# A hybrid decoder step on one core: first gMLP pair by plain products, output gates that leave PSUM without the heads, and work moved at two seams of the program

## The chip, the core and the metric

The kernel runs on one core of a Trainium2 chip. Times are device microseconds of one execution. The profile's names of the engines are used: PE (TensorE, matmuls and transposes), DVE (VectorE), ACT (ScalarE), POOL (GpSimd) and SP (SyncE, which here only issues DMAs). Each engine executes its instructions in the order of the program. "The clock" is the TensorE clock that was granted, which has two levels, 1.2 and 2.4 GHz, shown as 0.5 and 1.0.

## What is computed

One layer of a decoder trunk for 1024 prompt tokens and 64 sample tokens (8 sequences of 8), all in float32, D = 1024. The tokens are normalised and shifted by adaLN; one input projection feeds three branches; their gated outputs are projected, merged by sigmoid gates and projected once more. The reference, cut down:

```python
h = rmsnorm(x) * (1 + scale) + shift
z = h @ w_in + b_in                      # split into the columns named below
y_A = chunk_gmlp(u, v)                   # u * (causal mixing of rmsnorm(v)), 4 groups of 128 channels
y_B = sink_attention(q, k, v)            # window 128, 8 heads, 2 kv heads, sinks
y_C = sigmoid(o) * groupnorm(mlstm(conv(q, k), v, i, f))   # 4 heads of 128
y   = [y_b * silu(gate_b) for b in (A, B, C)]
m   = sum(sigmoid(merge_b) * (y_b @ w_b) for b in (A, B, C))
out = x + adaLN_gate * (m @ w_out)
```

It also returns the new keys and values of the window, the convolution's tail, the mLSTM states (C, n, m) and the normalised v of the samples.

## The kernel before, in words

**Products.** The 1088 tokens lie along the free dimension, the channels on the partitions, in 8 tiles of 128. A float32 product is made of three matmuls per tile of 128 rows, since each operand is split in a high and a low part (hh and hlo are h's; `w_split` and L124/L125 split weights: ACT casts the high part, DVE subtracts for the low one). A product over the whole of K = 1024 takes 24 matmuls for a piece of columns. PSUM results stand in three pools: pg (3 banks), pk (3) and pu (2). `gt` hands out temporary tiles of 128 x 384 from five buffers.

**Stage one, up to 349 us.** adaLN, h, then the mLSTM. While the four heads (`head`) run, PE fills its gaps with the products of the output gates: per head h, three chunks (384, 384 and 320 tokens) for o and three for g. `ev_o` (L785 to L787) takes Tanh of PSUM by ACT and multiplies it into `hn[h]`, the head's normalised output, by DVE. `ev_g` (L791 to L796) takes a second Tanh by ACT, then DVE multiplies the PSUM chunk itself into hn and the Tanh behind it. So an o chunk's bank is free once ACT has read it, and a g chunk's bank only when hn is there. At the end of a head DVE makes r out of dd (L736 to L740, with `rsqrt` L160 to L163 on POOL) and scales `num` by it (L741); PE transposes num, and ACT makes hn from that (L750). The states C_p and C_s go out by DMAs on POOL's queue (L694, L722), ahead of the rsqrt.

**Stage two, 359 to 600 us.** Nine `kv_tile`s, each a product of 24 matmuls of 256 columns into a pg bank, evicted by DVE into kn and vB (L921, L922). Then the attention: 20 steps (16 for prompts, 4 for samples), whose phases are interleaved on PE by hand (PLAN). Between them `filler` issues the products of the queries, of gMLP's v, and of `bg_chunk` (the silu gate of branch B, 12 chunks). A dict `tail` hangs more work on the steps: `t_first` (steps 0 to 3), `t_second` (11 to 18), `t_third` (22 to 25), `a_scale` (18: 36 ACT instructions that scale vn for the mixing), `mix(0)` to `mix(3)` (21, 22, 25, 25: causal mixing matrices times vn on PE, evicted by DVE, L1265).

**Stage three, 600 to 1079 us.** The gMLP pairs, their gates, the projections and merge gates. A pair is two column blocks of 128 of w_in times h. `seven` makes the 2 x 2 blocks (two halves of K, two halves of the tokens) of such a pair's four outputs by 7 products instead of 8, a Strassen scheme: products run over sums of halves of h (T tiles: `t_first` makes T5, `t_second` T6, `t_third` T4, and `t_in_place`, L1508 to L1514, T7 in the place of a half of h) and over sums of weight blocks (`comb`, L1366, by DVE). A product is 12 matmuls of 288 and 12 of 256 columns, two pieces of half the tokens. `items` is the list that runs here; `prepare` loads and splits the weights of an item five items ahead (LEAD). The first pair is item 0 to 7, behind `t_in_place`.

**Stage four, 1079 us to the end.** The output projection and the residual. It is not touched.

Of the kernel before, what the change touches and what calls it, by code (L numbers as in the profile page):

```python
# [38 lines left out]
def trunk_kernel(ctx: ExitStack, tc: tile.TileContext, I, O):  # L39
# [411 lines left out]
    with tc.tile_pool(name="cph", bufs=1, side="right", reuse_waits="tile") as c1:  # L451
# [166 lines left out]
        def head(h):  # L618
# [75 lines left out]
            nc.gpsimd.dma_start(O["C_p"][0, 0, h], Cp[:, 0:128])  # L694
# [14 lines left out]
            for b2 in range(2):  # L709
# [12 lines left out]
                nc.gpsimd.dma_start(O["C_s"][0, bs_, h].rearrange("b d e -> d b e"), Cs[b2][:, :, 0:128])  # L722
# [16 lines left out]
            rsqrt(r3, r2, 128)  # L739
# [76 lines left out]

    keep = ExitStack()
    k1 = keep.enter_context(tc.tile_pool(name="keep", bufs=1, side="right", reuse_waits="tile"))
    pe = ctx.enter_context(ExitStack())
    with tc.tile_pool(name="bph", bufs=1, side="right", reuse_waits="tile") as b1:  # L820
# [43 lines left out]
        ps = pk()  # L864
        tr(ps[:, 0:128], mT.rearrange("p a t -> p (a t)"))
        tr(ps[:, 128:160], mN.rearrange("p a h t -> p (a h t)"))
        mm(ps[:, 160:162], sel4.rearrange("p a h t -> p (a h t)"), snk4, True, True)
        V.tensor_copy(smask[:, 0:128], ps[:, 0:128])
        V.tensor_copy(smask[:, 160:192], ps[:, 128:160])
        scol = bt([128, 2], "scol")  # L870
        V.tensor_copy(scol, ps[:, 160:162])
        nscol = bt([128, 2], "nscol")
        V.tensor_scalar(nscol, scol, -1.0, None, ALU.mult)
# [32 lines left out]
        vB = slot("y7", [128, 9, 2, 64], name="vB")  # L906
# [103 lines left out]

        class Prompt:
# [12 lines left out]
            def s(self):  # L1024
# [60 lines left out]
        class Sample:  # L1085
# [19 lines left out]
            def s(self):  # L1105
# [108 lines left out]
        def t_next(x, q, k, kk, b, prev, to, c):  # L1214
            def v(t):
                return t[:, c].bitcast(F32)

            V.tensor_tensor(x, v(half(hh, kk, b)), v(TT[prev, k][0]), ALU.subtract)
            V.tensor_tensor(x, x, v(TT[prev, k][1]), ALU.subtract)
            V.tensor_tensor(x, x, v(half(hlo, kk, b)), ALU.add)  # L1220
# [560 lines left out]
```

## Time and profile before

| | |
|---|---|
| three runs | 1212.57, 1214.16, 1215.2 us, median 1214.16 |
| the profiled execution | 1213.49 us, its span 1211.8, so 1.7 us lie around the span |
| mean granted clock | 0.981 |
| busy: PE, DVE, ACT, POOL | 1162.9 us (96%), 790.1 (65%), 484.9 (40%), 77.5 (6%) |
| PE instructions | 8900 |

PE is busy nearly throughout, so a change counts by what it does to PE: fewer or more matmuls, less or more waiting, and the clock at which they run. What another engine does counts where PE waits for it. The rows behind the change show the waits.

### The profile page before, as it was taken

The numbers are of one execution on the slowest core, as the hardware profiler recorded it, in microseconds if no ns is written. First come the engines' busy times: TensorE is split into PE (matmuls) and PEld (weight loads), VectorE is DVE, ScalarE is ACT, GpSimd is POOL, SyncE is SP. The second block draws the span as 40 slices with busy tenths as digits, with TensorE's granted clock in tenths as the row PEclk, the third lists the DMA queues.
The fourth block names the chain that finished last, engine by engine and source line by source line (L and its number), as shares of the span: only waits on it lengthen the run. The fifth ranks groups of instructions, "written<-read, shape, count | busy, mean of one in ns | idle before, by whom it ended". The sixth has DMA issues, their size and how long they took to land.

```text
span 1211.8 us, 23137 instructions
## 1 busy us (share of the span) xinstructions
PE 1162.9 (96%) x8900; PEld 1113.5 (92%) x8900; DVE 790.1 (65%) x1887; ACT 484.9 (40%) x1215; POOL 77.5 (6%) x111
## 2 busy tenths in 40 slices
PE   5899999999979999999979999999999999999998
PEld 2699999999969998888878999999999999999998
DVE  3577877755465677776698784655766676668333
ACT  4443454433332377896243432333333343236000
POOL 2100001011022110010100000000000000000000
PEclk8999999999989999999988999999999999999999
DMA  9731222233222210213233246423544354466322
GB/s 306 230 88 36 73 67 79 58 106 102 80 66 68 69 40 23 71 41 99 61 87 106 81 129 203 149 82 96 169 111 112 110 167 127 127 205 195 99 90 74
DMA packets 150774, 129.74 MB, mean 107 GB/s; under 512 B 13614, under 2 KB 140214, under 8 KB 150649
## 3 DMA queue, kind: packets, MB, share of 16 engines
q1 hardware_dynamic: 142984, 118.96, 33.5%
q0 software_dynamic: 2240, 7.08, 1.7%
q10 hardware_dynamic: 5440, 2.23, 0.7%
q8 instruction: 70, 1.15, 0.4%
q14 instruction: 40, 0.32, 0.1%
HBM read 99.39 MB, written 29.82 MB: 107 GB/s over the span
## 4 chain that ended last, share of the span: by engine, by line
PE 50%; DVE 5%; ACT 3%; issue 1%; DMA 1%; SPq 0%; ACTq 0%; DVEq 0%
PE pg L85 21%; PE pk L85 17%; PE pu L85 12%; ACT vn L1255 1%; DVE prod L1372 1%; DMA raw<-in_w_out_dram 0%; ACT Sm L1044 0%; PE pu L89 0%; DMA mgr<-dmg 0%; DVE comb L1366 0%; DVE ml L1580 0%; DVE wo L1372 0%; DVE tx L1512 0%; ACT Sm L1052 0%; DVE sA L1265 0%
## 5 line engine op out<-in xcount | busy, mean ns | idle before, releaser
L85 PE MATMUL pg<-hl,hl 128*128 128x256 f32 (+3 forms) x904 | 278.1, 308 | 0.9 <-DVE hl L389 0.7
L85 PE MATMUL pg<-hh,hl 128*128 128x384 f32 (+1 forms) x912 | 238.9, 336 | 2.5 <-DVE hh L388 1.5
L85 PE MATMUL pg<-hl,hh 128*128 128x256 f32 (+1 forms) x1008 | 179.6, 285 | 0.1
L85 PEld LDWEIGHTS pg<-hl,hl 128*128 128x128 f32 x904 | 171.5, 190 | 4.0 <-DVE hl L389 2.7
L85 PEld LDWEIGHTS pg<-hh,hl 128*128 128x128 f32 x912 | 162.1, 190 | 6.8 <-DVE hh L388 2.9
L85 PEld LDWEIGHTS pg<-hl,hh 128*128 128x128 f32 x1008 | 151.9, 190 | 0.7 <-ACT pg L1194 0.3
L1371 ACT CAST prod<-raw 128x512 fp32r<-128x512 f32 x76 | 47.1, 620 | 124.7 <-PE pk L85 50.6
L85 PE MATMUL pg<-hh,prod 128*128 128x288 f32 (+1 forms) x400 | 85.1, 292 | 4.8 <-DVE prod L1372 2.7
L85 PE MATMUL pk<-hh,prod 128*128 128x256 f32 (+1 forms) x368 | 75.6, 286 | 2.5 <-ACT hh L813 2.5
L85 PEld LDWEIGHTS pg<-hh,prod 128*128 128x128 f32 x400 | 66.8, 191 | 5.3 <-DVE prod L1372 3.0
L1496 ACT ACTIVATE tt<-tt,bh 128x288 f32<-128x288 f32 x96 | 49.8, 521 | 46.1 <-DVE tt L1486 15.8
L1372 DVE TENSOR_TENSOR prod<-raw,prod 128x512 fp32r<-128x512 f32 x76 | 52.1, 687 | 24.1 <-ACT prod L1371 23.9
L1371 ACT CAST prod<-comb 128x512 fp32r<-128x512 f32 x64 | 39.3, 615 | 62.9 <-PE pk L85 26.5
L85 PEld LDWEIGHTS pk<-hh,prod 128*128 128x128 f32 x368 | 60.4, 189 | 4.0 <-ACT hh L813 2.8
L85 PE MATMUL pk<-tc,prod 128*128 128x256 f32 (+1 forms) x444 | 60.9, 286 | 0.0
L85 PE MATMUL pg<-yh,prod 128*128 128x288 f32 (+1 forms) x288 | 60.8, 289 | 0.0
L85 PE MATMUL pg<-tc,prod 128*128 128x288 f32 (+1 forms) x408 | 58.8, 294 | 0.0
L85 PE MATMUL pk<-yh,prod 128*128 128x256 f32 (+1 forms) x288 | 58.7, 284 | 0.0
L85 PE MATMUL pg<-hl,prod 128*128 128x288 f32 (+1 forms) x200 | 58.2, 291 | 0.0
L85 PEld LDWEIGHTS pk<-tc,prod 128*128 128x128 f32 x444 | 57.2, 188 | 0.9 <-DVE tt L1526 0.4
L85 PEld LDWEIGHTS pg<-tc,prod 128*128 128x128 f32 x408 | 55.2, 192 | 0.4 <-issue 0.4
L85 PE MATMUL pu<-hh,prod 128*128 128x288 f32 (+1 forms) x256 | 54.6, 292 | 0.0
(512 smaller groups left out, 2632.2 us busy)
## 6 DMA issues: line engine op xcount, KB each, us to landing
raw<-in_w_in_dram SPq DMA_DIRECT2D x124, 256.0 KB
adaraw<-in_ada_w_dram SPq DMA_DIRECT2D x16, 512.0 KB
stage<-dy SPq DMA_DIRECT2D x24, 272.0 KB
dmg<-tt SPq DMA_DIRECT2D x44, 144.0 KB
dmg<-tt SPq DMA_DIRECT2D x44, 128.0 KB
mprev<-dmg SPq DMA_DIRECT2D x32, 144.0 KB
xt<-in_x_prompt_dram SPq DMA_DIRECT2D x8, 512.0 KB
graw<-in_ada_w_dram SPq DMA_DIRECT2D x16, 256.0 KB
```

Of the source, the lines that this page charges most:

```text
L85: T.matmul(out, lhsT=lhsT, rhs=rhs, start=start, stop=stop)
L1255: S.activation(vn[g][:tn, n], vn[g][:tn, n], AF.Copy, scale=vq[:tn, n:n + 1])
L1371: S.copy(t[:, 0], x)
L1372: V.tensor_tensor(t[:, 1], x, t[:, 0].bitcast(F32), ALU.subtract)
L1496: S.activation(x, x, AF.Tanh, bias=bh[:, b:b + 1], scale=0.5)
```

## The change

It has six parts.

1. In `head`, the DMAs of C_p and C_s are issued behind the rsqrt, and the rsqrt is issued at high priority.
2. The output gates no longer touch hn in a chunk. `ev_o` writes its Tanh to a full-width tile `w`. `ev_g` takes Tanh and, new, Identity (z, with the bias) of the PSUM chunk by ACT; DVE multiplies (Tanh + 1) into z and (w + 1) * z into w, all in SBUF. One full-width DVE instruction per head, `hn *= w` over 1088 columns, comes last (`lastc` is the last head's).
3. `t_first(0)` to `t_first(3)` move from the attention's steps 0 to 3 to behind kv tiles 1, 3, 5 and 7, with the order that they come after `lastc`. The masks' three PE instructions and their copies move behind kv tile 4.
4. `a_scale` is cut in four, a quarter (9 ACT instructions) at each of steps 18 to 21, each behind the newest softmax Exp; `mix` runs at steps 21, 22, 22, 23 instead of 21, 22, 25, 25, `t_third(0)` at 24, and the other three `t_third`s leave the attention.
5. The last chunk of branch B's gate (24 matmuls of 320 columns) leaves the filler and runs ahead of the last output phase of the attention. Its bank is kept, and ACT and DVE evict it in the last phase (`last_gate`).
6. The first gMLP pair is made by `plain`: its four outputs of half the tokens by 24 matmuls of 288 and 24 of 256 columns each, with neither weight sums nor T tiles. T4 for k = 1 to 3 (`t_late`) and `t_in_place` come behind its first products. The second pair is the first by `seven`. Slots are exchanged accordingly.

The diff, cut to its core:

```diff
@@ head
-            nc.gpsimd.dma_start(O["C_p"][0, 0, h], Cp[:, 0:128])
...
-            rsqrt(r3, r2, 128)
+            with tc.high_priority():
+                rsqrt(r3, r2, 128)
+            nc.gpsimd.dma_start(O["C_p"][0, 0, h], Cp[:, 0:128])
+            for b2 in range(2):
+                nc.gpsimd.dma_start(O["C_s"][0, 4 * b2:4 * b2 + 4, h].rearrange("b d e -> d b e"), Cs[b2][:, :, 0:128])
@@ gates of the heads
-            To = []
+            w = slot(f"y{h % 2}", [128, NT], name="wog")
             def ev_o(ci, c0, n, ps):
-                t = gt(n, "to")
-                S.activation(t, ps[:, :n], AF.Tanh, bias=bh[:, CO + h:CO + h + 1], scale=0.5)
-                V.scalar_tensor_tensor(hn[h][:, c0:c0 + n], t, 1.0, hn[h][:, c0:c0 + n], ALU.add, ALU.mult)
+                S.activation(w[:, c0:c0 + n], ps[:, :n], AF.Tanh, bias=bh[:, CO + h:CO + h + 1], scale=0.5)
             def ev_g(ci, c0, n, ps):
-                t = gt(n, "tg")
+                t, z = gt(n, "tg"), gt(n, "zg")
                 S.activation(t, ps[:, :n], AF.Tanh, bias=bh[:, CG + h:CG + h + 1], scale=0.5)
-                p = gt(n, "pg")
-                V.scalar_tensor_tensor(p, ps[:, :n], cols[:, CG + h:CG + h + 1], hn[h][:, c0:c0 + n], ALU.add, ALU.mult)
-                V.scalar_tensor_tensor(hn[h][:, c0:c0 + n], t, 1.0, p, ALU.add, ALU.mult)
+                S.activation(z, ps[:, :n], AF.Identity, bias=cols[:, CG + h:CG + h + 1], scale=1.0)
+                V.scalar_tensor_tensor(z, t, 1.0, z, ALU.add, ALU.mult)
+                V.scalar_tensor_tensor(w[:, c0:c0 + n], w[:, c0:c0 + n], 1.0, z, ALU.add, ALU.mult)
+            lastc = V.tensor_tensor(hn[h], hn[h], w, ALU.mult).ins
@@ attention
-        tail = {0: lambda: t_first(0), 1: lambda: t_first(1), 2: lambda: t_first(2), 3: lambda: t_first(3), 11: lambda: t_second(0), 13: lambda: t_second(1), 17: lambda: t_second(2),
-                18: seq(lambda: t_second(3), a_scale), 20: a_load, 21: lambda: mix(0),
-                22: seq(lambda: mix(1), lambda: t_third(0)), 23: lambda: t_third(1),
-                25: seq(lambda: mix(2), lambda: mix(3), lambda: t_third(2), lambda: t_third(3))}
+        tail = {11: lambda: t_second(0), 13: lambda: t_second(1), 17: lambda: t_second(2),
+                18: seq(lambda: t_second(3), a_norm, lambda: a_scale(0)), 19: lambda: a_scale(1), 20: seq(lambda: a_scale(2), a_load),
+                21: seq(lambda: a_scale(3), lambda: mix(0)), 22: seq(lambda: mix(1), lambda: mix(2)),
+                23: lambda: mix(3), 24: lambda: t_third(0)}
         for n in range(9):
             kv_tile(hl, n)
+            if n % 2 and n < 8:
+                with tc.issue_after(lastc):
+                    t_first(n // 2)
+            if n == 4:
+                masks()
...
+                    if ph == "y" and i - d == len(steps) - 1:
+                        filler(1 << 30)
+                        gemm_T(wview(hl, 0, 256)[:, :, 128:256], wview(hl, 1, 256)[:, :, 128:256], 8, hh, hlo,
+                               lambda ci, c0, n, ps: kept.append((c0, n, ps)), (2,))
@@ last phase
+    def plain(cols2, final):
...
+        def run(i, h):
+            for j in range(2):
+                c = part_(h, j)
+                ps = bank()[:, :CUT[j][1]]
+                for k in range(8):
+                    three(ps, st[i, k // 4], k % 4, hh[k][:, c], hlo[k][:, c], k == 0, k == 7)
+                x = tt(j)
+                with tc.high_priority():
+                    S.copy(x, ps)
+                final(i, h, j, x)
...
-    items += [act(t_in_place, *((k,) for k in range(4)))] + it[0][:5] + it[1][:1] + it[0][5:]
+    items += [(None, last_gate)] + it[0][:2] + [behind(t_late, 1, 1)] + it[0][2:4] + [behind(t_late, 3, 2, 3), act(t_in_place, *((k,) for k in range(4)))] + it[0][4:]
```

What stands where on the engines. First PE at the end of the last head, before (num and nst feed the heads' transposes, cso the convolution's tail; pg GEMMs with hh_..., hl 128x320 are the last gate chunk, those with hl, hh_... 128x256 are the kv tiles):

```order
L85 MATMUL pg<-hh_568,hl 128x320
L85 MATMUL pg<-hl_569,hl 128x320
L85 MATMUL pg<-hh_568,hl 128x320
L89 MATMUL pk<-ident,num 128x128 x8
L89 MATMUL pk<-ident,num 128x64
L89 MATMUL pk<-ident,nst 36x128
L89 MATMUL pk<-ident,cso 27x128 x8
L85 MATMUL pg<-hl,hh_250 128x256 x2
L85 MATMUL pg<-hl,hl_251 128x256
```

The same place of the changed kernel:

```order
L85 MATMUL pg<-hl,hh_268 128x256 x2
L85 MATMUL pg<-hl,hl_269 128x256
L85 MATMUL pg<-hl,hh_312 128x256 x2
L89 MATMUL pk<-ident,num 128x128 x8
L89 MATMUL pk<-ident,num 128x64
L85 MATMUL pg<-hl,hl_313 128x256
L85 MATMUL pg<-hl,hh_328 128x256 x2
L85 MATMUL pg<-hl,hl_329 128x256
```

The transposes of num now stand behind the first 8 matmuls of kv tile 0, and those of nst and cso inside kv tile 1 and behind.

DVE at that place, before (r and num belong to the last head; tx and tc to `t_first`; L125 splits weights):

```order
L814 TENSOR_TENSOR tc<-tx,tc 128x544
L1209 TENSOR_TENSOR tx<-tx 128x544
L1207 TENSOR_TENSOR tx<-hh_312 128x544
L125 TENSOR_TENSOR hl<-raw,hl 128x512
L1208 TENSOR_TENSOR tx<-hl_313 128x544
L125 TENSOR_TENSOR hl<-raw,hl 128x512
L740 TENSOR_TENSOR r_2871<-r_2874,dd 128x9
L125 TENSOR_TENSOR hl<-raw,hl 128x512
L814 TENSOR_TENSOR tc<-tx,tc 128x544
L1209 TENSOR_TENSOR tx<-tx 128x544
L741 TENSOR_TENSOR num<-num,r_2871 128x9x128
```

The changed kernel, from r to hn (zg and wog are the tiles z and w of the gates):

```order
L735 TENSOR_TENSOR r_2868<-r_2868,sq 128x9
L719 TENSOR_TENSOR Cs<-Cs,pk 128x4x128 x2
L742 TENSOR_TENSOR r_2868<-r_2871,dd 128x9
L743 TENSOR_TENSOR num<-num,r_2868 128x9x128
L795 SCALAR_TENSOR_TENSOR zg<-tg,zg 128x384
L796 SCALAR_TENSOR_TENSOR wog<-wog,zg 128x384
L125 TENSOR_TENSOR hl<-raw,hl 128x512
L795 SCALAR_TENSOR_TENSOR zg<-tg,zg 128x320
L125 TENSOR_TENSOR hl<-raw,hl 128x512
L796 SCALAR_TENSOR_TENSOR wog<-wog,zg 128x320
L125 TENSOR_TENSOR hl<-raw,hl 128x512
L799 TENSOR_TENSOR hn<-hn,wog 128x1088
```

Nothing of `t_first` stands between r and num any more. It stands behind hn, in two groups (T5 for k = 0 and 1, then for k = 2 and 3), and ahead of the first eviction of a kv tile; this is the end of that stretch, some 15 instructions on:

```order
L1226 TENSOR_TENSOR tx<-hh_328 128x544
L1227 TENSOR_TENSOR tx<-hl_329 128x544
L857 MEMSET neg 128x1
L859 MEMSET mf 128x128
L867 MEMSET mT 128x128
L870 MEMSET mN 32x128
L874 MEMSET sel_3723 4x128
L880 MEMSET smask 128x32
L881 MEMSET smask 128x32
L1228 TENSOR_TENSOR tx<-tx 128x544
L942 TENSOR_TENSOR kn<-pg,bkb 128x128
L943 TENSOR_TENSOR vB<-pg,bkb 128x128
```

The first eviction of a kv tile (kn and vB, from a pg bank) now stands behind 24 instructions that follow hn: 13 of `t_first`, one L125, the copy of nrowo and nine memsets. Before, it followed the last instruction of hn behind eight memsets and a cast.

PE at the start of the last phase, before (WT, vn are `mix`; ots, vB, vcn, Sx belong to the attention's last steps; prod is the first split weight of the first pair):

```order
L85 MATMUL pg<-hh_568,hl 128x320
L89 MATMUL pu<-ident,ots 64x128
L85 MATMUL pu<-vB,PTs 128x64
L85 MATMUL pu<-vcn,PTs 32x64 x4
L89 MATMUL pu<-ident,ots 64x128
L85 MATMUL pk<-WT,vn 128x128 x8
L85 MATMUL pk<-WTs,vn 128x64
L85 MATMUL pk<-WT,vn 128x128 x8
L85 MATMUL pk<-WTs,vn 128x64
L85 MATMUL pg<-hh_250,prod 128x288
L85 MATMUL pg<-hl_251,prod 128x288
```

The changed kernel, first ahead of the kept chunk, then behind its 24 matmuls:

```order
L89 MATMUL pu<-ident,Sx 128x128
L89 MATMUL pu<-ident,Sx 64x128
L85 MATMUL pk<-WT,vn 128x128 x8
L85 MATMUL pk<-WTs,vn 128x64
L89 MATMUL pu<-ident,ots 64x128
L85 MATMUL pu<-vB,PTs 128x64
L85 MATMUL pu<-vcn,PTs 32x64 x4
L85 MATMUL pg<-hh_250,hl 128x320
L85 MATMUL pg<-hl_251,hl 128x320
```

```order
L85 MATMUL pg<-hl_569,hl 128x320
L85 MATMUL pg<-hh_568,hl 128x320
L89 MATMUL pu<-ident,ots 64x128
L85 MATMUL pg<-hh_250,prod 128x288
L85 MATMUL pg<-hl_251,prod 128x288
```

The last ots now follows 24 matmuls behind vcn instead of directly, all mixing lies ahead of it, and the first product follows it at once.

## Rows read from the trace of the kernel before

**Rows 1.** What PE waited for over the whole span: the PSUM pool and line of the waiting instruction, the engine and tile waited for; us in total, times, longest us. Lines above and between are left out.
```profile
PE pk L89 <- DVE num L741: 6.2, 1, 6.2
...
PE pg L85 <- DVE prod L1372: 2.7, 1, 2.7
PE pu L89 <- DVE ots L1143: 2.5, 1, 2.5
PE pk L85 <- ACT hh L813: 2.5, 1, 2.5
PE pk L85 <- DVE QT L1007: 2.1, 1, 2.1
PE pg L85 <- ACT prod L1371: 2.1, 1, 2.1
...
PE pu L89 <- ACT Sm L1052: 1.8, 1, 1.8
...
PE pk L85 <- DVE hl L814: 1.0, 1, 1.0
```

**Rows 2.** Windows of 2 us around the end of the last head: start and end, length, then busy us (instructions) of PE, PE's weight loads, DVE, ACT and POOL, the granted clock, the share of the DMA engines, GB/s.
```profile
354.00:356.00 2.00, 0.64 (x3) 0.67 (x4) 2.00 (x3) 0.91 (x2) 0.00 (x0) 0.50 0.68 229
356.00:358.00 2.00, 1.93 (x9) 1.18 (x7) 1.05 (x3) 1.35 (x3) 0.00 (x0) 0.50 0.49 124
358.00:360.00 2.00, 1.70 (x9) 1.39 (x9) 2.00 (x5) 1.31 (x5) 1.11 (x2) 0.50 0.27 76
360.00:362.00 2.00, 2.00 (x11) 2.00 (x11) 2.00 (x7) 0.85 (x2) 0.86 (x2) 0.50 0.22 46
362.00:364.00 2.00, 2.00 (x14) 2.00 (x13) 0.61 (x6) 0.00 (x0) 1.91 (x6) 0.65 0.52 159
```

**Rows 3.** The same view, a window of 16 us over the kv tiles.
```profile
364.00:380.00 16.00, 16.00 (x141) 15.56 (x139) 6.48 (x26) 0.59 (x1) 3.64 (x7) 1.00 0.22 73
```

**Rows 4.** DVE's and PE's timelines at the end of the last head: start us, us, engine, line, operation, tiles and shapes, and in brackets how long the engine was idle before and who released it.
```profile
343.61 0.17 DVE L907 MEMSET kn<- 64x128 f32 x1
...
348.80 0.72 DVE L1209 TENSOR_TENSOR tx<-tx 128x544 f32<-128x544 f32 x1
349.44 0.72 DVE L1207 TENSOR_TENSOR tx<-hh 128x544 f32<-128x544 f32 x1
...
353.87 1.35 DVE L741 TENSOR_TENSOR num<-num,r 128x1152 f32<-128x1152 f32 x1
```
```profile
355.37 2.23 PE L89 MATMUL pk<-ident,num 128*128 128x128 f32 x9 [6.24 <-DVE num L741]
```

**Rows 5.** POOL's timeline there.
```profile
346.73 0.76 POOL L722 DMA_DIRECT2D out_dram<-Cs  x1 [8.35 <-DVE Cs L720]
...
348.04 1.83 POOL L163 TENSOR_TENSOR r<-r,mhalf 128x9 f32<-128x9 f32 x1
```

**Rows 6.** Windows of 2 us at the start of the last phase (the columns of rows 2).
```profile
602.00:604.00 2.00, 2.00 (x13) 1.77 (x11) 2.00 (x6) 0.00 (x0) 0.00 (x0) 0.59 0.15 25
604.00:606.00 2.00, 2.00 (x11) 1.88 (x11) 2.00 (x7) 0.42 (x1) 0.00 (x0) 0.56 0.00 0
...
610.00:612.00 2.00, 0.32 (x2) 0.00 (x0) 1.97 (x4) 0.00 (x0) 0.00 (x0) 0.50 0.00 0
612.00:614.00 2.00, 0.99 (x4) 0.99 (x5) 1.89 (x4) 1.17 (x2) 0.00 (x0) 0.50 0.00 0
614.00:616.00 2.00, 2.00 (x10) 2.00 (x9) 2.00 (x4) 0.18 (x1) 0.00 (x0) 0.50 0.00 0
...
636.00:638.00 2.00, 1.01 (x3) 0.80 (x4) 1.30 (x3) 0.00 (x0) 0.00 (x0) 0.62 0.00 0
638.00:640.00 2.00, 2.00 (x11) 2.00 (x11) 1.12 (x3) 0.53 (x1) 0.00 (x0) 0.50 0.00 0
640.00:642.00 2.00, 2.00 (x10) 2.00 (x10) 1.93 (x5) 1.15 (x3) 0.00 (x0) 0.50 0.00 0
642.00:644.00 2.00, 2.00 (x13) 2.00 (x13) 1.07 (x4) 0.23 (x1) 0.00 (x0) 0.67 0.21 46
```

**Rows 7.** PE's timeline of one product of the first pair, 12 matmuls of 288 and 12 of 256 columns, and the start of the product behind it.
```profile
623.11 1.75 PE L85 MATMUL pg<-tc,prod 128*128 128x288 f32 x12
624.69 1.58 PE L85 MATMUL pk<-tc,prod 128*128 128x256 f32 x12
626.11 0.30 PE L85 MATMUL pg<-hh,prod 128*128 128x288 f32 x1
```

**Rows 8.** The timelines of ACT (ACTq is its DMA issue) and of DVE where the last phase starts.
```profile
601.37 0.42 ACT L1150 COPY ys<-pu 64x64 f32<-64x64 f32 x2 [0.17 <-PE pu L89]
601.82 0.37 ACTq L1153 DMA_DIRECT2D dy<-ys  x1
...
608.80 0.61 ACT L1371 CAST prod<-raw 128x512 fp32r<-128x512 f32 x1
```
```profile
612.27 0.69 DVE L1372 TENSOR_TENSOR prod<-raw,prod 128x512 fp32r<-128x512 f32 x1
```

**Rows 9.** Groups of ACT instructions by line between 100 and 349 us: instructions, busy us, mean ns of one, and what ended the idle time before them; then the window of 230 to 349 us, where the gates run (the columns of rows 2).
```profile
L635 ACT ACTIVATE E<-E,colsT 128x128 f32<-128x128 f32 (+1 forms) x36 | 10.8, 382 | 15.1 <-POOL E L630 15.1
...
L793 ACT ACTIVATE tg<-pg,bh 128x384 f32<-128x384 f32 (+1 forms) x10 | 5.5, 558 | 16.0 <-PE pg L85 16.0
```
```profile
230.00:349.00 119.00, 119.00 (x788) 113.06 (x786) 66.21 (x164) 41.07 (x118) 15.76 (x23) 1.00 0.27 84
```

More of the change, by code (lines that the diff above doesn't have):

```diff
@@ L815, in t_split, with t_tile, t_next, v @@
         return t0, t1
+    def t_tile(tag):
+        t = slot(tag, [128, 2, HT], F32R, name="tc")
+        return t[:, 0], t[:, 1]
+    def t_next(x, q, k, kk, b, prev, to, c):
+        def v(t):
+            return t[:, c].bitcast(F32)
+        V.tensor_tensor(x, v(half(hh, kk, b)), v(TT[prev, k][0]), ALU.subtract)
+        V.tensor_tensor(x, x, v(TT[prev, k][1]), ALU.subtract)
+        V.tensor_tensor(x, x, v(half(hlo, kk, b)), ALU.add)
+        t_split(x, to[0][:, c], to[1][:, c])
+        TT[q, k] = to
+    T4S = ("y6", "m0", "m4", "m1")
+    kept = []
     keep = ExitStack()
@@ L1212, in t_first @@
                 TT[q, k] = (half(hh, kk, b), half(hlo, kk, b))
[L1214 to L1220, printed above, removed]
-            t_split(x, to[0][:, c], to[1][:, c])
-            TT[q, k] = to
         def t_second(k):
@@ L1246, in a_load, with a_norm @@
             A["gvo"] = bt([64, 4, 128], "gvo", tag="QT", bufs=3)
-        def a_scale():
+        def a_norm():
             vr = bt([128, 9], "vr", tag="rr", bufs=2)
@@ L1252, in a_scale @@
             rsqrt(vq, vr, 512)
-            for g in range(4):
+            A["vq"] = vq
+        def a_scale(g):
+            vq = A["vq"]
+            with tc.issue_after(newS[0]):
                 for n, (t0, tn) in enumerate(TILES):
@@ L1303, in fill_steps @@
             order += [("a", s, n) for s in range(2) for n in range(9)]
-            order += [("b", f, ci) for f in range(4) for ci in range(3)]
+            order += [("b", f, ci) for f in range(4) for ci in range(3)][:-1]
             for kind, a, c in order:
@@ L1370, in w_split, with behind, run @@
         t = tile if tile is not None else w2.tile([128, 2, 512], F32R, tag="prod", bufs=6, name="prod")
-        S.copy(t[:, 0], x)
-        V.tensor_tensor(t[:, 1], x, t[:, 0].bitcast(F32), ALU.subtract)
-        return t
+        a = S.copy(t[:, 0], x)
+        b = V.tensor_tensor(t[:, 1], x, t[:, 0].bitcast(F32), ALU.subtract)
+        splits.append((a.ins, b.ins))
+        return t
+    splits = []
+    def behind(f, n, *ks):
+        def run(_):
+            with tc.issue_after(splits[n][0]), tc.issue_after(splits[n][1]):
+                for k in ks:
+                    f(k)
+        return (None, run)
     def wk(t, part, k, n=128):
@@ L1489, in seven, with prep, first @@
         return [(lambda q=q: prep(q), lambda t, q=q: run(q, t)) for q in order]
+    def plain(cols2, final):
+        st = {}
+        def prep(i, j):
+            return w_split(raw_load(kv(w_in[:, cols2[i]:cols2[i] + 128])[:, 4 * j:4 * j + 4]))
+        def run(i, h):
[8 more added lines that the diff above has]
+                final(i, h, j, x)
+        def first(i, j, t):
+            st[i, j] = t
+            if j:
+                run(i, 1)
+        out = [(lambda i=i, j=j: prep(i, j), lambda t, i=i, j=j: first(i, j, t)) for i in range(2) for j in range(2)]
+        return out + [(None, lambda _, i=i: run(i, 0)) for i in range(2)]
     Q7 = (1, 6, 7, 5, 3, 2, 4)
@@ L1515, in t_in_place, with t_late @@
         TT[7, k] = t_split(x, half(hh, k, 1), half(hlo, k, 1))
+    def t_late(k):
+        x = y2[0].tile([128, 2, HT], F32, tag="yh1", name="tx")[:, 0]
+        t_next(x, 4, k, k + 4, 0, 6, t_tile(T4S[k]), slice(0, HT))
     def y_tiles(f):
```

70 lines of the change are left out of this document (40 added, 30 removed).

## Prediction

> **What bounds the kernel now.** I read the page first: PE is busy for 96% of the span, so the time is PE's work plus what PE waits, plus what it loses at the lower clock. The list of PE's waits comes next, since it says which waits the six edits can touch [rows 1]. Outside the start (adaLN, untouched) nearly all of the waiting stands at two seams. At the end of the last head PE waits 6.2 us for num. At the start of the last phase it waits 2.5 us for ots, then 2.1 and 2.7 us for the two parts of prod, then 2.5 and 1.0 us for hh and hl, the T7 that is made in place. In between are 1.8 us for Sm and waits for QT, of which the longest has 2.1 us. The reader is to see that a seam costs more than its wait. In the 2-us windows behind the num wait the clock stands at 0.5 although PE is busy [rows 2]; the same holds behind the waits at 598 to 614 us and at 636 us [rows 6].
>
> I price the loss of a window as busy time times (1 - granted clock). At the first seam that is 0.64 x 0.5 + 1.93 x 0.5 + 1.70 x 0.5 + 2.00 x 0.5 + 2.00 x 0.35 = 3.8 us [rows 2]. With the wait of 6.2 and 0.4 more for nrowo it costs 10.5 us. At the second the nine windows give 0.82 + 0.88 + 0.16 + 0.50 + 1.00 + 0.38 + 1.00 + 1.00 + 0.66 = 6.4 us [rows 6], and the five waits 2.5 + 2.1 + 2.7 + 2.5 + 1.0 = 10.8 [rows 1], together 17.2 us. So 27.7 us stand at the seams; everywhere else the edits can only add PE work or break something.
>
> **Plain products.** This is the sure cost. A product by `seven` (12 matmuls of 288 and 12 of 256 columns) runs from 623.11 to 626.11 us, 3.00 us [rows 7]. A pair by seven takes seven, 21.0 us. `plain` makes four outputs of 24 + 24 matmuls each, which is eight such units, 24.0 us. Cost: **+3.0 us** on PE, certain, as PE is the bound there.
>
> **Second seam.** Before, DVE makes T4 (`t_third`), the evictions of the mixing, T7 and the weight sums all at once while PE stands. In the change the first products need neither T tiles nor sums; the mixing is ahead, and 24 matmuls of 320 columns cover the last ots. What is left is the way from the last ots transpose to the first product: ACT copies ys (0.42 us), issues its DMA (0.37) and only then casts the first weight (0.61) [rows 8]; with the semaphores between, about 1.6 us. The third matmul also needs DVE's low part, 0.69 us [rows 8], of which some 0.45 us lie behind the two matmuls that can run. So PE still waits about 2.1 us. Does that take the clock? The trace has both sides: the QT wait of 2.1 us [rows 1] is followed by a granted clock of 1.00, and the ots wait of 2.5 us by windows of 0.59 and 0.56 [rows 6]. I take no loss, being at the nearer row, and keep 1.7 us (those two windows) for the range.
>
> After that, T7, the remaining T4 and the sums have the 24 us of `plain` and the first products of the second pair as cover. Product 7 is the sixth of that pair, so it starts some 24 + 15 = 39 us behind the start of the phase. By the order on DVE, with the durations of the profile, I find T7 done about 5 us before that. If that cover were gone, the price is the old one: 2.5 + 1.0 us of waiting and about 3.0 us of clock (the last four windows) [rows 1, 6].
>
> Balance of the last phase: 17.2 saved, less 2.1 left, less 3.0 for plain: **-12.1 us**, between -9 and -12.5.
>
> **First seam.** The edits take all reasons for the num wait away: r no longer stands behind `t_first` on DVE (instructions of 0.64 us from start to start [rows 4]), the rsqrt (1.83 us) no longer behind a DMA issue of 0.76 on POOL [rows 5], and PE can go on with gate chunks and with kv tiles while hn is made, because the gates' banks leave by ACT alone. I put num at about 346.6 and PE at its transposes at 349.4, so they don't wait.
>
> But the same order puts a new queue on DVE. kv tile 3 needs a pg bank, the three banks hold tiles 0 to 2, and the first of them is evicted by kn and vB. On DVE these stand behind hn *= w, and that behind hn, which ACT has copied at about 352.8. Then come: hn *= w, near L741's 1.35 us [rows 4], say 1.3; 13 of `t_first` and one L125 at 0.64, 9.0; ten small ones at the memset's 0.17 [rows 4], 1.7. The sum is 12.0, so kn starts at about 364.8. PE meanwhile has the 9 transposes, three kv tiles at 16.0 / 141 = 0.113 us a matmul [rows 3], less the 8 matmuls that it did first, and the transposes of nst and cso: 349.4 + 1.1 + 64 x 0.113 + 1.2 = 359. It waits **5.9 us** there, nearly as long as before, but with three kv tiles done. Tile 3 starts at 365; before, PE starts the kv tiles at 359.9 at half clock, and reaches tile 3 at 370.1. That gains 5.1 us. Behind a wait that long the clock falls by all rows here, and gives back 1.7 us (the two windows behind the ots wait [rows 6]) to 3.8 (those behind num [rows 2]). I take 3, nearer the longer wait: **-2 us**. The bounds are 0.5 and -5, and -10.5 with no new wait at all.
>
> **The gates.** Twelve Identity instructions are new on ACT, priced at a Tanh of the same chunk, 0.56 us, 6.7 us in all. ACT is busy for 41 of the 119 us in which the gates run, and waits for PE before most of them [rows 9]; so I cost it at nothing. The cover is that idle time. DVE keeps two instructions per chunk and gets one of full width for three of chunk width.
>
> **a_scale and mix.** The 36 ACT instructions of vn stand ahead of a softmax in one lump; spread behind the newest Exp, they free the Sm wait of 1.8 us [rows 1]. I take **-1 us**, between -2 and +2: mix now meets the softmax steps on DVE, but three `t_third`s leave it. The masks and the C DMAs of other heads I cost at nothing; none of PE's waits names them.
>
> **Sum.** -12.1 - 2 - 1 = -15.1. From the profiled execution's 1213.49 that gives 1198.4; the median of the runs is 0.7 higher, so I forecast 1199.
>
> **Rivals.**
> A. The new wait at kv tile 3 doesn't come, because DVE is there sooner (hn is ready earlier than I place it, or the instructions overlap more). For: DVE was idle for 9.5 of the 16 us over the kv tiles [rows 3]. Against: the order is fixed and 24 instructions stand between. Then the first seam gives 10.5 instead of 2: 1190.5.
> B. The 2.1 us at the second seam are longer, and the clock falls there too, or T7 is late. For: the sides at 2.1 and 2.5 us are close. Price 1.7 of clock plus about 0.5, or 6.5 with T7's: 1201 to 1205.
> The Trainium skill, page "TensorE: Matmul & The Clock Gate", section "What's actually happening", says that the chip judges activity in windows that run free of the kernel's start. By that rule the same wait may keep the clock in one place and lose it in another, so the edge between 2.1 and 2.5 us would not be sharp, and the sum could be 1199 or 1201 from run to run. No run here shows this yet.
> C. The first seam gives nothing: the wait at kv tile 3 is 1 to 2 us longer (the bias of kn is loaded behind weight blocks on SP), with the full 3.8 us of clock: 5.1 - 1.5 - 3.8 is about 0: 1201.
> D. Slower than before: the pg banks of the gate chunks. Their release now needs two ACT instructions in a row. ACT's queue also holds the E of the heads, for which ACT waits 15.1 us on POOL [rows 9]; a Tanh or an Identity behind such an E holds its bank as long. PE was busy in all of the 119 us [rows 9], so every delay there is pure loss. It needs 15.1 us over 12 chunks, above 1.3 us for each, to eat the whole gain. Against: the Tanh stood in that queue before as well, and PE waited for none of them [rows 1].
> On the extra pass the Trainium skill speaks against the change: page "VectorE: DVE Perf Modes", section "Rules for kernel authors", advises to read a matmul's result from PSUM in place, and to copy it out first only for many operations; here one DVE instruction reads it. By that advice the pass is cost without return, 6.7 us of ACT; by the rows ACT has the room and the return is the bank.
>
> **How the numbers follow.** Forecast 0.50 (1195 to 1200), A 0.20, B 0.12, C 0.09, D 0.05 (1217 and more), and 0.04 for a gain lost in several small ways to about no change. The range 1189 to 1207 holds the first four cases with their bounds and leaves out about 0.15. Some 0.2% (2.4 us) is what a measurement of this kernel can tell from no change. Faster by more than that: 0.91; within: 0.04; slower: 0.05.
>
> **What would show it.** Right: no wait for num in the list of PE's waits; a wait of pg for kn or vB (DVE) of 4 to 8 us near 359 to 365, with a clock of 0.5 behind it; one wait of about 2 us for prod (ACT) at the start of the last phase, with the clock at 1.00 behind it; 24 us for the first pair; no waits for hh or hl near 630; no Sm wait. Wrong: a wait for tg or zg (ACT) on pg between 230 and 349 (D); a wait for hh, hl, tc or comb near 640 (B); PE's busy time up by clearly more than 3 us, at a mean clock that has not risen from 0.981.

## The result, and the profile after

The changed kernel takes 1200.68 us (four runs, 1200.06 to 1201.65) where the kernel before took 1213.37 (1212.28 to 1215.2): a ratio of 0.9895, 95% interval 0.9878 to 0.9912, or 12.7 us less. The forecast was 1199 in a range of 1189 to 1207.

The page of the profiled execution (1201.65 us, span 1199.9) has the same picture as before, a PE that is busy nearly throughout:

```profile
PE 1160.6 (97%) x8924; PEld 1112.5 (93%) x8924; DVE 775.9 (65%) x1846; ACT 489.0 (41%) x1225; POOL 82.3 (7%) x111
```

The waits of PE over the whole span (us in total, times, longest), the ones behind the start, answer to [rows 1]:

```profile
PE pg L85 <- DVE vB L943: 5.3, 1, 5.3
...
PE pg L85 <- ACT mh L1643: 2.7, 1, 2.7
PE pk L85 <- DVE QT L1028: 2.1, 1, 2.1
PE pk L89 <- DVE QT L1028: 1.8, 1, 1.8
PE pg L85 <- ACT prod L1394: 1.6, 1, 1.6
...
PE pu L85 <- DVE tt L1504: 0.8, 1, 0.8
...
PE pg L85 <- ACT gsb L1699: 0.7, 1, 0.7
PE pu L89 <- ACT Sm L1075: 0.7, 1, 0.7
```

The waits for num, ots, hh and hl are gone. In their place stand one wait of 5.3 us for vB, which is kv tile 3 waiting for a bank, and one of 1.6 us for prod. Three more are new or longer, and I had none of them in my sum: tt, gsb, and mh at the output projection, 2.7 us where it was 1.8.

**First seam after.** DVE's and PE's timelines between the last head's product (hn) and kv tile 3:

```profile
351.92 1.29 DVE L799 TENSOR_TENSOR hn<-hn,wog 128x1088 f32<-128x1088 f32 x1
353.13 0.72 DVE L1226 TENSOR_TENSOR tx<-hh 128x544 f32<-128x544 f32 x1
...
362.65 0.67 DVE L1228 TENSOR_TENSOR tx<-tx 128x544 f32<-128x544 f32 x1
363.25 0.27 DVE L942 TENSOR_TENSOR kn<-pg,bkb 128x128 f32<-128x128 f32 x1
363.45 0.27 DVE L943 TENSOR_TENSOR vB<-pg,bkb 128x128 f32<-128x128 f32 x1
```
```profile
348.76 1.24 PE L89 MATMUL pk<-ident,num 128*128 128x128 f32 x9
...
363.87 0.77 PE L85 MATMUL pg<-hl,hh 128*128 128x256 f32 x2 [5.27 <-DVE vB L943]
```

PE transposes num at 348.76 without a wait (349.4 in my sum), DVE's queue then runs from hn to kn in 11.3 us (12.0), and PE waits 5.27 us (5.9). The windows of 2 us behind it (columns of rows 2) show what the wait costs besides:

```profile
362.00:364.00 2.00, 0.13 (x1) 0.16 (x1) 2.00 (x13) 0.64 (x1) 1.70 (x4) 0.60 0.66 189
364.00:366.00 2.00, 2.00 (x10) 2.00 (x11) 2.00 (x8) 0.59 (x1) 2.00 (x3) 0.50 0.23 73
366.00:368.00 2.00, 2.00 (x11) 2.00 (x11) 1.92 (x5) 0.06 (x1) 2.00 (x2) 0.50 0.02 4
368.00:370.00 2.00, 2.00 (x15) 2.00 (x14) 0.63 (x3) 0.15 (x1) 1.65 (x3) 0.70 0.04 8
```

That is 1.0 + 1.0 + 0.6 = 2.6 us at the lower clock, against 3.8 in [rows 2].

**Second seam after.** PE's and ACT's timelines, then the windows of 2 us:

```profile
598.67 0.27 PE L89 MATMUL pu<-ident,ots 128*64 128x128 f32 x1
600.50 0.40 PE L85 MATMUL pg<-hh,prod 128*128 128x288 f32 x1 [1.57 <-ACT prod L1394]
```
```profile
598.98 0.42 ACT L1173 COPY ys<-pu 64x64 f32<-64x64 f32 x2 [1.27 <-PE pu L89]
599.43 0.37 ACTq L1176 DMA_DIRECT2D dy<-ys  x1
599.84 1.14 ACT L1394 CAST prod<-raw 128x512 fp32r<-128x512 f32 x2 [0.44 <-ACT ys L1173]
```
```profile
600.00:602.00 2.00, 1.30 (x5) 1.07 (x6) 1.44 (x3) 2.00 (x5) 0.00 (x0) 0.83 0.11 16
602.00:604.00 2.00, 2.00 (x11) 2.00 (x10) 1.99 (x4) 1.36 (x3) 0.54 (x1) 0.50 0.80 226
604.00:606.00 2.00, 2.00 (x14) 2.00 (x14) 1.21 (x3) 0.64 (x2) 0.00 (x0) 0.82 1.03 279
```

The chain is the one of the forecast: ys, its DMA issue, the cast. But behind a wait of 1.6 us the clock falls to 0.5, which I had not expected below 2.1 us; it costs 1.30 x 0.17 + 1.0 + 0.4 = 1.6 us.

**Where the time went.** Three landmarks that both programs have cut an execution in pieces: the small transposes at the end of the start (R, at 77.9 us before), the matmul behind the 2.1 us wait for QT (466.24), and the first matmul of the first pair (609.47). The start, which no edit touches, ends between 76.1 and 79.2 us in the executions of this study, so a span by itself says little below 2 us. Each row is one execution, the profiled one.

| execution | R to QT | QT to first product | from there to the end of the span |
|---|---|---|---|
| before | 388.3 | 143.2 | 602.3 |
| the change | 386.3 | 137.7 | 599.4 |
| difference | -2.0 | -5.6 | -2.9 |

With 1.4 us of the start that makes the 11.9 us between the spans.

### The profile page after: what moved, and what is told of

Same layout as the page of the kernel before. It is cut to its first block, busy times and chain, and to the rows that moved or that the text cites. A ratio compares the mean times of both kernels' runs of the same rounds, so it can differ in the third digit from the quotient of the medians.

```text
span 1199.9 us, 23127 instructions
## 1 busy us (share of the span) xinstructions
PE 1160.6 (97%) x8924; PEld 1112.5 (93%) x8924; DVE 775.9 (65%) x1846; ACT 489.0 (41%) x1225; POOL 82.3 (7%) x111
## 4 chain that ended last, share of the span: by engine, by line
PE 87%; DMA 5%; DVE 4%; SPq 3%; ACT 1%; issue 1%; ACTq 0%; DVEq 0%
PE pg L85 49%; PE pk L85 22%; PE pu L85 13%; PE pk L89 2%; DMA adaraw<-in_ada_w_dram 2%; SPq L251 1%; PE pu L89 1%; DMA mrow<-in_ada_b_dram 1%; DMA raw<-in_w_in_dram 1%; DMA mgr<-dmg 1%; DMA gbs<-drow 0%; SPq L267 0%; DMA raw<-in_w_out_dram 0%; DVE hl L125 0%; DVE wo L1395 0%
## 5 line engine op out<-in xcount | busy, mean ns | idle before, releaser
L85 PE MATMUL pk<-hh,prod 128*128 128x256 f32 (+1 forms) x400 | 80.9, 285 | 0.0
L85 PEld LDWEIGHTS pk<-hh,prod 128*128 128x128 f32 x400 | 65.1, 188 | 0.8 <-DVE tt L1512 0.4
L1394 ACT CAST prod<-comb 128x512 fp32r<-128x512 f32 x60 | 36.9, 614 | 54.2 <-PE pk L85 23.7
L85 PE MATMUL pu<-hh,prod 128*128 128x288 f32 (+1 forms) x280 | 57.7, 287 | 0.0
L85 PE MATMUL pk<-hl,prod 128*128 128x256 f32 (+1 forms) x200 | 56.8, 284 | 0.0
L85 PE MATMUL pk<-tc,prod 128*128 128x256 f32 (+1 forms) x408 | 56.2, 287 | 0.0
L85 PE MATMUL pg<-tc,prod 128*128 128x288 f32 (+1 forms) x396 | 55.7, 290 | 0.0
L85 PEld LDWEIGHTS pk<-tc,prod 128*128 128x128 f32 x408 | 52.7, 188 | 1.3 <-issue 0.9
```

What stands on the lines that cost most here:

```text
L85: T.matmul(out, lhsT=lhsT, rhs=rhs, start=start, stop=stop)
L1394: a = S.copy(t[:, 0], x)
```

## The experiments

Twelve kernels ran, in three groups of four, each group on one chip with runs of the kernel before. The landmarks of all are in the table behind the last one.

**1. t_first out of DVE's way.** Is the new wait at kv tile 3 DVE's queue?

```diff
                 if n % 2 and n < 8:
-                with tc.issue_after(lastc):
+                with tc.issue_after(kvdone[0]):      # newest eviction of a kv tile
                     t_first(n // 2)
```

> The changed kernel with one order altered: each t_first comes behind the newest eviction of a kv tile instead of behind the last head's product. Theory (the new wait of 5.3 us at kv tile 3 is DVE's queue: 13 instructions of t_first stand ahead of kn): kn then waits only for the load of its bias, which was issued at 356.8 us and lands near 359, so the wait falls to about 1 us and the stretch at half clock behind it goes; 4 us of wait and 2.6 us of clock, about 1194 to 1195 us. Rival (the wait is the bias's or hn's, and DVE's queue only looks like it): the wait stays near 5 us and the time at 1200 to 1201.

Measured: 1196.71 us, ratio 0.9856 (0.9834 to 0.9879). The waits of PE that touch the seam, and the window where the change stood still:

```profile
PE pk L89 <- ACT kst L969: 1.8, 1, 1.8
...
PE pg L85 <- DVE vB L945: 0.9, 1, 0.9
```
```profile
358.00:361.00 3.00, 2.12 (x19) 1.95 (x18) 1.21 (x8) 0.00 (x0) 1.08 (x4) 1.00 0.27 71
```

The wait falls from 5.3 to 0.9 us and the clock stays at 1.00; the piece from R to QT is 382.2 us, 4.1 less than the change. DVE's queue it was. Of the 6 to 6.6 us that I expected, about 2 went into a new wait for kst, the copies of k, whose norm on DVE now stands among the instructions of t_first. In this execution the clock fell behind the QT wait, which the change's didn't, and stayed at 1.00 behind the prod wait, where the change's fell; at 1.7 us each the two cancel.

**2. The gates as they were**, with everything else of the change (t_first still behind the last head's product). The diff is part 2 of the change, undone.

> The changed kernel with the gates of the heads as they were: a g chunk's bank leaves PSUM through hn. The rest stays. Theory of my prediction (the gates' banks let PE go on, the second new order only moves the wait): PE doesn't wait for num, but the first kv tile waits for a bank until hn is made, about 3 us from 351.5 to 354.5, and then tile 3 waits little, since DVE is then ahead of PE; some 1 to 3 us slower than the change, 1202 to 1204. Rival A (the gates are what frees the seam): the wait of about 6 us is back with 3.8 us of clock, 1207 or more. Rival B (the gates give nothing): 1200 to 1201.

Measured: 1197.97 us, ratio 0.9863 (0.9843 to 0.9883), 2.7 us below the change, which ran in another group; from R to QT it takes 382.3 us, 4.0 less. None of my three cases held. PE's waits there:

```profile
PE pk L89 <- ACT hn L752: 1.1, 2, 0.8
...
PE pg L85 <- DVE pg L797: 0.7, 1, 0.7
...
PE pg L85 <- DVE vB L944: 0.6, 1, 0.6
...
PE pk L89 <- DVE num L743: 0.6, 2, 0.3
```

PE waits in pieces of under 1 us, and the clock stays up. A likely reason, not tried by itself, stands in DVE's order: in this kernel 6 instead of 13 instructions of t_first stand ahead of the first kn, since the second half of t_first was put behind it. So this run alone doesn't price the gates; experiment 11 does.

**3. The last output phase inside the kept chunk's product.** Is the prod wait ACT's way over ys?

```diff
-                        gemm_T(... kept.append((c0, n, ps)), (2,))
+                        last = gemm_T_steps(... kept.append((c0, n, ps)), (2,))
+                        for _ in range(5):
+                            next(last)
+                        getattr(steps[i - d], ph)()
+                        for _ in last:
+                            pass
+                        continue
```

> The changed kernel with the last output phase of the attention put inside the kept chunk's product (behind 5 of its 8 parts, 15 of 24 matmuls) instead of behind it. Theory (the wait at the start of the last phase is ACT's way from the last ots over ys and its DMA issue to the first cast): that way then lies beside 9 matmuls of 1.2 us, the wait of 1.6 us falls to under 0.6 and the clock doesn't fall behind it, so 1.0 of wait and 1.6 of clock are gained: about 1198. Rival (the first weight's load or another reader holds the cast): no change, 1200 to 1201.

Measured: 1200.76 us, ratio 0.9889 (0.9871 to 0.9907), no difference that the time can show. PE's timeline, and the windows of 2 us:

```profile
601.28 0.40 PE L85 MATMUL pg<-hh,prod 128*128 128x288 f32 x1 [0.25 <-ACT prod L1400]
```
```profile
602.00:604.00 2.00, 1.99 (x15) 2.00 (x16) 1.91 (x4) 2.00 (x5) 0.48 (x1) 1.00 0.36 90
604.00:606.00 2.00, 2.00 (x19) 2.00 (x18) 1.46 (x3) 1.06 (x3) 0.06 (x1) 1.00 1.11 323
```

At the place it does what the theory says: 0.25 us of wait instead of 1.57, the clock at 1.00, 1.1 us less from QT to the first product and 1.3 from there to the end. Its start was 1.5 us longer than that of the change's execution, which hides most of the 2.4 between these two executions. By time alone the rival's 1200 to 1201 came out; the theory is shown at the place only.

**4 and 5. Seven products for the first pair.** In 4, T7 is made behind the pair's first product and the late T4 behind its fourth; in 5, three of the four T4 are made in the attention again.

```diff
-    it = [plain((0, 1024), gmlp_pair(0))]
-    it += [seven(...) for g in range(1, 4)]
+    it = [seven(...) for g in range(4)]
...                                          # the order of items, as said above
# 5 only
-                23: lambda: mix(3), 24: lambda: t_third(0)}
+                23: lambda: mix(3), 24: lambda: t_third(0), 25: seq(lambda: t_third(1), lambda: t_third(3))}
```

> The changed kernel with the first pair by seven products again, T7 and the late T4 made right behind its first weights; everything ahead of the last phase as in the change. Theory (plain products cost 3.0 us and pay for it by covering T7, T4 and the weight sums on DVE): 3.0 us less PE work, but waits for prod, hh and hl of 5 to 8 us with 3 to 4 us of clock, 1205 to 1209. Rival (the mixing ahead and the late T4 do it, and plain is only a cost): 1197 to 1199.

> The first pair by seven products as in the run before, 1218.9 us, whose wait of 8.0 us for T4 and 5.8 for hh (T7) were more than forecast. Here three of the four T4 are made in the attention again, as in the kernel before the change; T7 stays behind the first weights. Theory (plain's worth is the cover for T7, T4 and the sums on DVE): the T4 waits fall to 2 or 3 us and those for T7 stay or shrink, 1205 to 1212, still slower than the change by clearly more than plain's 3.0 us of PE. Rival (only the late T4 made seven slow): 1198 to 1201.

Measured: 4 takes 1218.89 us, ratio 1.0043 (1.0026 to 1.0059); 5 takes 1211.67, ratio 0.9979 (0.9968 to 0.9990). PE's waits of 4 and of 5:

```profile
PE pg L85 <- ACT tc L814: 8.0, 2, 4.5
PE pk L85 <- ACT hh L814: 5.8, 2, 3.8
```
```profile
PE pk L85 <- ACT hh L814: 5.8, 2, 3.8
...
PE pg L85 <- ACT prod L1394: 4.5, 1, 4.5
```

With T4 late, seven waits 8.0 us for T4 (tc) and 5.8 for T7 (hh). With T4 early the T4 wait is gone, but those instructions stand at the seam: ACT's last casts of tc run from 601.45 us, the cast of prod follows them at 602.83, and prod waits 4.5. Against the change run in the same group (experiment 6), 5 is 8.2 us slower. The pieces are best read against the change's first execution, since neither lost the clock behind the QT wait: 2.8 us more from QT to the first product and 6.7 behind it. So plain costs 3.0 us of PE and, against the better of these two arrangements of seven, returns some 11, by covering T7, T4 and the sums. The arrangement of the kernel before, T7 ahead of the first product, was not tried with the rest of the change; there the T7 waits were 3.5 us and not 5.8, so plain's return may be some 2 us smaller than this.

**6. The change itself once more**, beside 5, 7 and 8.

> The changed kernel itself, unaltered, beside the next three on one chip: 1200 to 1201 us. It tells how far its time moves from one group of runs to the next, against which the others are read.

Measured: 1203.43 us, ratio 0.9909 (0.9895 to 0.9923): 2.8 us more than in the first group. Its profiled execution shows where most of it can lie. Windows of 4 us behind the QT wait, first of this execution, then of the change's first one:

```profile
464.00:468.00 4.00, 4.00 (x23) 4.00 (x22) 1.73 (x4) 1.40 (x5) 1.18 (x1) 0.57 0.00 0
```
```profile
464.00:468.00 4.00, 4.00 (x37) 4.00 (x36) 2.79 (x8) 1.35 (x5) 0.87 (x1) 1.00 0.00 0
```

Both have the same wait of 2.1 us ahead of that window. In one the clock falls to the lower level behind it, 4.0 x 0.43 = 1.7 us, in the other it doesn't. The chip may have a part in it too; no run here separates that. One program thus moves by 2 to 3 us, and differences below that are read from pieces, not from times.

**7. Both alterations, 1 and 3, in one kernel.**

> t_first behind the evictions of the kv tiles and the last output phase inside the kept chunk's product, both alterations of before together. If the two gains are each their own (4 us of the first by its runs; of the second 1.1 us of wait and 1.6 of clock, which its trace shows at the place and its time doesn't): 1194 to 1195 us. If the second gives its gain back later, as a longer wait in the last phase or at the output projection: 1196 to 1197.

Measured: 1197.29 us, ratio 0.9870 (0.9850 to 0.9890), 6.1 us faster than the change in its own group, with intervals that don't touch. The pieces give both gains, 382.6 and 136.5 us. The last piece is 599.6: the mh wait is 3.5 us there, and a window of 55 us around it has a mean clock of 0.94. The same place costs 1.2 us less of wait and 1.6 less of clock in experiment 3 (2.25 us, and 0.83 over the 10 us behind it). So the second case held within 0.3 us, a gain that is given back at the output projection; why mh comes later there isn't shown. Kernels 1 and 7 beat both kernels of this case.

**8. All of t_first behind the ninth kv tile.**

```diff
-            if n % 2 and n < 8:
+            if n == 8:
                 with tc.issue_after(kvdone[0]):
-                    t_first(n // 2)
+                    for k in range(4):
+                        t_first(k)
```

> As the kernel with both alterations, but all of t_first behind the ninth kv tile's eviction, so that DVE has nothing but evictions and norms while PE runs the kv tiles. With t_first behind tiles 1, 3, 5 and 7 PE still waited 1.8 us for the copies of k (kst), 0.8 for sel and 0.9 for vB. If these come from t_first on DVE, they go, up to 2.6 us less than its twin, 1192 to 1193; if t_first then meets the queries' work at the start of the attention on DVE, QT is late and it is the same or slower, 1195 to 1198.

Measured: 1204.74 us, ratio 0.9916 (0.9903 to 0.9929). The reason is one wait:

```profile
PE pk L89 <- ACT kst L969: 7.0, 1, 7.0
```

The 16 instructions of t_first now stand ahead of and among the last norm of k, beside the first work for the queries, and PE waits 7.0 us; from R to QT it takes 389.9 us, more than before the change. Standing close together these instructions made PE wait 6.2, 5.3 and 7.0 us in three places (the kernel before, the change, here); between the evictions the longest wait is 2.2 us (kst in experiment 12).

**9. No kept chunk**: the last chunk of branch B's gate goes back into the filler (part 5 undone).

> The changed kernel with the last chunk of branch B's gate back in the filler, so nothing covers the last ots on PE. Theory (the chunk's 24 matmuls of 3.5 us are the cover of the last ots): the wait for ots is back with 2 to 3 us, the wait for prod stays at 1.6 us behind it, the clock falls for longer; 3 to 5 us slower than the change's 1200.7 to 1203.4 of two groups, 1204 to 1207. Rival (the mixing ahead is what matters): no slower than 1 us.

Measured: 1204.21 us, ratio 0.9928 (0.9911 to 0.9945). PE's waits:

```profile
PE pu L89 <- DVE ots L1166: 2.6, 1, 2.6
...
PE pg L85 <- ACT prod L1391: 1.6, 1, 1.6
```

The ots wait is back with 2.6 us, and the piece from QT to the first product is 140.4 us, 2.7 more than in the change's first execution, which kept the clock behind QT as this one did. The chunk's 24 matmuls were the cover. The time alone can't tell this kernel from the change in its second group (1203.43 us).

**10. The scaling in one lump** (the first half of part 4 undone; `mix` and `t_third` stay where the change has them).

> The changed kernel with the 36 ACT instructions of the scaling in one lump at step 18 again. Theory: the Sm wait of 1.8 us is back where the change has 0.7, so 1 us slower than the change, inside what two groups of runs differ by. Rival (no part in it, or mix then waits for vn): 0, or 2 us and more with a new wait for vn on PE.

Measured: 1202.31 us, ratio 0.9909 (0.9892 to 0.9925), no difference to the change in its second group. PE's wait for Sm is back, and a window of 10 us at the second seam:

```profile
PE pu L89 <- ACT Sm L1075: 1.8, 1, 1.8
```
```profile
596.00:606.00 10.00, 8.24 (x61) 7.38 (x61) 7.62 (x19) 5.12 (x13) 0.54 (x1) 1.00 0.24 56
```

The 1.1 us of Sm, which the piece from QT to the first product shows too (138.8 against 137.7), is the worth of cutting the scaling. What it is worth to have `mix` earlier was not tried by itself. By chance this execution kept the clock behind the prod wait of 1.6 us and behind the mh wait of 2.2, where both of the change lost it; its last piece is 595.1 us, with the same code as the change's 599.4, and two falls of 1.7 are most of that.

**11. Gates as before, with both alterations of 7.**

> The changed kernel with the gates as before, t_first behind the kv evictions and the last output phase inside the kept chunk's product. Theory (the gates' new way out of PSUM is worth nothing once t_first is out of DVE's way): the same time as its twin with the new gates, 1196 to 1199. Rival (the gates do help there): 2 us or more slower than the twin, 1199 to 1201.

Measured: 1199.15 us, ratio 0.9885 (0.9867 to 0.9904), 1.9 us above its twin, in another group. From R to QT it takes 384.2 where the twin takes 382.6; its waits for hn (1.1 us) and for the gates' bank (0.7) are those that the new gates avoid. So by these two executions the gates are worth some 1.6 us once t_first is out of the way. The times alone, at the edge between the two cases, don't settle that.

**12. One edit on the kernel before**: t_first behind the kv evictions, as in 1.

> The kernel before with one edit: t_first behind the evictions of kv tiles 1, 3, 5 and 7, nothing else. Theory (DVE's queue of t_first is the whole first seam; the gates, the masks and the order of the DMAs add nothing to it): no wait for num, short waits for hn and for the gates' banks of 2 to 3 us in all, no half clock, the landmark of the query wait 5 to 7 us earlier, 1207 to 1209. Rival (the gates' banks are needed too): half of it or less, 1210 and more.

Measured: 1209.60 us, ratio 0.9966 (0.9954 to 0.9978). PE's waits:

```profile
PE pk L89 <- ACT kst L948: 2.2, 1, 2.2
...
PE pk L89 <- ACT hn L750: 1.1, 2, 0.8
PE pg L85 <- DVE pg L795: 0.7, 1, 0.7
...
PE pk L89 <- DVE num L741: 0.2, 1, 0.2
```

The num wait falls from 6.2 to 0.2 us by this edit alone, and R to QT takes 383.5 us, 4.8 less than before, more than twice what parts 1 to 3 of the change give there. The medians differ by 3.7 us. The time lies between my two cases, 0.6 us above the theory's, and this execution lost the clock behind the QT wait, which the profiled one of the kernel before kept.

| execution | R to QT | QT to first product | to the end | median us |
|---|---|---|---|---|
| 1, t_first behind kv | 382.2 | 138.1 | 597.6 | 1196.71 |
| 2, old gates | 382.3 | 137.5 | 599.9 | 1197.97 |
| 3, last output inside | 386.6 | 136.6 | 598.1 | 1200.76 |
| 4, seven, T4 late | 385.7 | 137.7 | 615.5 | 1218.89 |
| 5, seven, T4 early | 386.3 | 140.5 | 606.1 | 1211.67 |
| 6, the change again | 386.1 | 139.2 | 599.8 | 1203.43 |
| 7, both | 382.6 | 136.5 | 599.6 | 1197.29 |
| 8, t_first in a lump | 389.9 | 137.1 | 596.0 | 1204.74 |
| 9, no kept chunk | 386.0 | 140.4 | 599.4 | 1204.21 |
| 10, scaling in a lump | 386.0 | 138.8 | 595.1 | 1202.31 |
| 11, old gates and both | 384.2 | 138.1 | 599.5 | 1199.15 |
| 12, before with one edit | 383.5 | 144.4 | 602.2 | 1209.60 |

## Why the prediction was right, and where it was not

**First seam: right in mechanism and in size.** I forecast that the num wait is replaced by one of 5.9 us for kn and vB at kv tile 3, with 3 us of clock, for a gain of 2. Measured are 5.3, 2.6 and 2.0 us, the last against one execution of the kernel before; the seven profiled executions that share this stretch with the change gain 1.7 to 2.6. Rival A (the wait doesn't come) was what an edit of the order could still bring, not what the change does: experiment 1 gets 4.1 us more. I credited all of parts 1 to 3 with taking the old wait away, and that was wrong: experiment 12 does it with one. The order of the C DMAs and the rsqrt needs no edit; there POOL's program has the rsqrt ahead of the DMAs of C_s without one.

**Plain products: right.** PE's instructions rise from 8900 to 8924, the 24 of one product of 3.00 us [rows 7], and experiments 4 and 5 show the cover, worth more than I said: with T7 where they have it, not 3.5 us of its waits return, as in the kernel before, but 5.8, and T4 or prod besides.

**Second seam: the right mechanism, mis-sized.** The waits at the seam came out as forecast, 1.8 us left of 10.8 (I said 2.1). The term of -12.1 and the -1 for the scaling make -13.1; the two pieces behind QT give -8.5, so 4.6 us of the forecast gain are missing. I had not counted three things. First the step "I take no loss, being at the nearer row": the clock fell behind the wait, 1.6 us, which was rival B's price. Then two waits that I didn't see coming in the last phase, tt (0.8; 0.5 to 1.7 in the kernels with plain that have it, none in 4 and 5) and gsb (0.7). And the mh wait at the output projection, 0.9 us longer, with the lower clock behind it in this execution:

```profile
1090.00:1100.00 10.00, 7.31 (x58) 6.81 (x56) 9.48 (x23) 5.10 (x12) 0.00 (x0) 0.98 0.82 254
1100.00:1110.00 10.00, 9.85 (x74) 9.85 (x75) 6.05 (x15) 2.44 (x7) 0.00 (x0) 0.85 0.40 130
```

That is 0.1 + 1.5 = 1.6 us, where the kernel before kept 1.00 behind its mh wait. Listed so, they are 5.6 us, or 5.3 less the 0.3 that prod waits less; that is 0.7 more than is missing, and I can't place it. Why mh comes later in the order of `plain` was not tried.

That the time lies only 1.7 us above the forecast is in part luck: the pieces gain 10.5 us where the sum had 15.1, but a start that is shorter by 1.4 us, which no edit touches, gives some of it back in the profiled pair, and the median of the changed kernel's runs lies 1.0 us below its profiled one.

**Scaling: right**, 1.1 us at the Sm wait. A second wait for QT is 0.4 us longer (1.8 where it was 1.4), but it stands at 493 us, ahead of the scaling, and is the same in experiment 10.

**Rivals.** B happened in part (the clock; T7 was in time). C didn't. D, the gates' extra ACT pass, didn't (and what it needed was 15.1 / 12 = 1.26 us a chunk, not above 1.3): no wait for tg or zg on PE between 230 and 349 us, and PE is busy in 118.98 of these 119 us. On the rule of the Trainium skill ("VectorE: DVE Perf Modes", "Rules for kernel authors": read PSUM in place unless many operations follow) the runs are divided: as the change stands, the gates in place are as fast or faster (experiment 2); with t_first out of the way the copy returns about 1.6 us (experiments 7 and 11).

## What to carry to other kernels

A wait that is removed by moving its cause is found again where the cause now stands: count the instructions of the moved block ahead of the next instruction that frees a buffer, and put the block behind that one instead. Work that only DVE does (operands for a cleverer product) was free here only where PE had plain work to cover it; a first product with more matmuls and no operands to make can be worth several times its price. Before a gain of 2 us is believed, cut the execution at landmarks, compare pieces, and look in each for a fall of the clock that the other doesn't have.

## What the hardware showed that I had not expected

The clock behind a short wait isn't decided by the wait's length alone. The same 2.1 us wait for QT stands in all fourteen profiled executions. Nine keep a clock of 1.00 behind it, the kernel before and the change among them; in five it falls to 0.50 (experiments 1, 6, 8, 11 and 12). The prod wait of 1.6 us lost the clock in both executions of the change and in experiments 2 and 4, and kept it in 1 and 10, with much the same code around it. Mh waits of 2.1 to 2.4 us lost it in experiments 1, 3, 5 and 9 and kept it in 8, 10 and 12. Here are the windows behind the QT wait in experiment 12, and behind the prod wait in experiment 6:

```profile
464.00:468.00 4.00, 4.00 (x24) 4.00 (x23) 2.03 (x4) 0.97 (x4) 0.76 (x1) 0.60 0.00 0
```
```profile
604.00:606.00 2.00, 2.00 (x12) 2.00 (x11) 1.99 (x4) 1.26 (x4) 0.54 (x1) 0.56 0.91 250
606.00:608.00 2.00, 2.00 (x12) 2.00 (x12) 1.50 (x3) 0.74 (x2) 0.00 (x0) 0.58 1.02 293
```

Each such fall costs 1.6 to 1.7 us here. The Trainium skill, page "TensorE: Matmul & The Clock Gate", section "What's actually happening", says that activity is judged in windows that run free of the program; these executions agree with it. An edge that I had read between 2.1 and 2.5 us from one execution was no edge. No run here shows how to choose on which side a wait falls. To take the wait away is what worked: with 0.25 us of wait for prod the clock stayed at 1.00 in all four executions that have it (experiments 3, 7, 8 and 11).
